# Moving the full-precision rows of odd blocks to ScalarE and the filter-half sums to VectorE in a diffusion transformer block

## Chip, cores and metric

The kernel runs on one core of one Trainium2 chip. The metric is the device time of one execution in microseconds, taken as the median of several runs.

## What is computed

One block of a hybrid diffusion model on 512 latent tokens and 256 context tokens of width 1024: an adaptive norm, one input projection whose columns feed four token mixers (differential attention, neighbourhood attention, pooling and a long convolution with generated filters), an output projection with a gate, and then a mixture of 16 experts with two of them per token. The change touches the norm with its modulation, and the generation of the convolution's filters:

```python
mod_l = jnp.split(jax.nn.silu(c) @ lp['ada_w'] + lp['ada_b'], 6, axis=-1)
mod_c = jnp.split(jax.nn.silu(c_ctx) @ lp['ada_w'] + lp['ada_b'], 6, axis=-1)
hl = rmsnorm(xl, lp['norm1_g']) * (1.0 + sc1_l) + sh1_l
hc = rmsnorm(xc, lp['norm1_g']) * (1.0 + sc1_c) + sh1_c
aq_l, ak_l, av_l, bq_l, bk_l, bv_l, pool_l, hy_l = split_cols(hl @ lp['w_in'])
...
h = jnp.sin(HY_SIN_FREQ * (h @ w2 + b2))
h = (h @ w3 + b3).reshape(L, HY_ORDER, 2, HY_CH)
h = h * jnp.exp(-t_norm[:, None, None, None] * deltas)
return h * lax.rsqrt(jnp.sum(h * h, axis=(0, 2), keepdims=True) + EPS)
```

The two halves of a filter (forward and backward) are needed as their sum and their difference, since the spectrum of the two-sided filter is built from those.

## The kernel before

Products are made to nearly full float32 precision from two reduced-precision parts: a number x is kept as hi (x rounded to fp32r) and lo (x minus hi, in fp32r), and a product takes three matmuls, hi by hi, hi by lo and lo by hi (`mm3`, lines 77 to 79). `split` (lines 72 to 74) makes the parts: ScalarE copies to hi, VectorE subtracts for lo.

The first 90 us hold these stages. `ada1` streams eight 1 MB pieces of the modulation weights through TensorE (line 355), moves each result out (line 358, ScalarE and VectorE in turn), and turns it into columns in the PSUM tile `pm` (line 360). From `pm`, VectorE makes the shift `md` and the scale `m1` (lines 362 to 364). `filters` generates the long convolution's filters for two orders n: a small network, the decay (line 287), the sums of squares `sqs` (line 292), then the sum `s` and the difference `d` of the two halves (line 301: GpSimd adds, VectorE subtracts), their splits `hs` and `hd`, the norm `ss` over partitions (line 306) with its root and reciprocal, and the transform to the spectrum (line 318, tiles `fk`), whose results VectorE scales (line 323) and GpSimd combines (lines 328 to 331).

`modulate` takes the normed tokens in eight blocks of 128 columns, first for the latents (`ht`, 512 wide), then for the context (`hc`, 256 wide). For each block TensorE transposes into a PSUM bank `xt` (line 373; four banks go round), ScalarE writes hi = scale * x + shift from PSUM (line 379), VectorE writes the same in full precision to the tile `hf` from the same bank (line 380; two `hf` buffers), and lo = hf - hi is made by VectorE in even blocks and by GpSimd in odd blocks (line 381). The first projection group (tiles `pl`, latents, and `pc`, context, lines 488 to 504) takes these parts block by block. The splits of its weights (`wh` on ScalarE, `wl` on VectorE, 2048 wide) lie on the same engines.

The order of the instructions on each engine isn't that of the text. The program is built with a scheduler that simulates a timeline and puts what it finds ready in front, so matmuls of the projection (written after `modulate`) run between the filter's and the transposes, and a changed duration or engine can change the order of other instructions, later ones too. What it puts on an engine then runs in that fixed order.

After the first 90 us come the rest of the projection with the convolution, the attentions, the output projection, the routing, and from about 460 us the experts, whose weights (line 1605, 1 MB pieces) stream in while TensorE works.

Of the kernel before, what the change touches and what calls it, by code (L numbers as in the profile page):

```python
# [11 lines left out]
AF = mybir.ActivationFunctionType  # L12
ALU = mybir.AluOpType
# [33 lines left out]
def tile_hybrid_block(ctx, tc, ins, out):  # L47
    nc = tc.nc
    V, A, G, T, SY = nc.vector, nc.scalar, nc.gpsimd, nc.tensor, nc.sync
# [19 lines left out]
    def f(ap):  # L69
        return ap.bitcast(F32)  # L70

    def split(hi, lo, src, eng=None):
        A.copy(hi, src)  # L73
        (eng or V).tensor_sub(lo, src, f(hi))  # L74
# [119 lines left out]
    def xbank(name, shape=(128, 512)):  # L194
        return psx.tile(list(shape), F32, tag="x", name=name, bufs=2)

    def jbank(name, shape=(128, 512)):
        return psx.tile(list(shape), F32, tag="j", name=name, bufs=2)

    def tbank(name, shape=(128, 512)):  # L200
        return pst.tile(list(shape), F32, tag="t", name=name, bufs=4)
# [66 lines left out]
    def filters():  # L268
        p = xbank("f1", (64, 512))
# [5 lines left out]
        p = xbank("f2", (64, 512))  # L275
# [5 lines left out]
        for n in range(2):  # L281
            hh = fw([128, 4, 2, 256], F32, "hh")
            sqs = fw([128, 2, 256], F32, "sqs")
            for j in range(4):
                p = xbank("f3")
# [12 lines left out]
            hsp = {nm: [fw([128, 4, 256], F32R, f"h{nm}{q}") for q in range(2)] for nm in "sd"}  # L298
            for nm, op in (("s", ALU.add), ("d", ALU.subtract)):
                t = fw([128, 4, 256], F32, "hsd")  # L300
                (G if nm == "s" else V).tensor_tensor(t, hh[:, :, 0, :], hh[:, :, 1, :], op=op)
                split(hsp[nm][0], hsp[nm][1], t)
            yield 1
            ss = xbank("ss", (128, 256))
# [6 lines left out]
            for ft in range(2):  # L311
                fwd = dftf[ft]
                pk = []
                for m in range(4):
                    p = xbank("fk", (128, 256))
# [11 lines left out]
                k = fw([128, 4, 256], F32, "kt")  # L327
# [14 lines left out]
    md = cst.tile([128, 16, 2], F32, name="md")  # L342
    m1 = cst.tile([128, 8, 2], F32, name="m1")
# [23 lines left out]
    def modulate(xs, vi):  # L367
        nt = len(xs)
        n = nt * 128
        for k in range(8):  # L370
            p = tbank("xt")
            for j in range(nt):
                T.transpose(p[:, j * 128:(j + 1) * 128], xs[j][:, k * 128:(k + 1) * 128], ident)
            hf = t1.tile([128, 512], F32, tag="hf", name="hf", bufs=2)
            if vi == 0:
                hi, lo = hT[0][k // 4][:, k % 4, :], hT[1][k // 4][:, k % 4, :]
            else:
                hi, lo = hC[0][:, k, :], hC[1][:, k, :]
            A.activation(hi, p[:, :n], AF.Identity, scale=m1[:, k, vi:vi + 1], bias=md[:, k, vi:vi + 1])
            V.tensor_scalar(hf[:, :n], p[:, :n], m1[:, k, vi:vi + 1], md[:, k, vi:vi + 1], op0=ALU.mult, op1=ALU.add)  # L380
            (G if k % 2 else V).tensor_sub(lo, hf[:, :n], f(hi))
            yield

    flt = filters()

    def some(g, n):
# [10 lines left out]
    hC = [hslot(4 + q, [128, 8, 256], f"hc{q}") for q in range(2)]  # L397
    xs_c = load_x(cd, 2, W1.ld[7])
    run(modulate(xs_l, 0))
    norm_x(xs_c)  # L400
    run(modulate(xs_c, 1))
    t1_s.close()
    sbank = tbank
# [691 lines left out]
    p = jbank("b16", (128, 16))  # L1095
# [123 lines left out]
    for k in range(2):  # L1219
        V.scalar_tensor_tensor(jg(oh[:, k]), jg(erk), float(k), gm.to_broadcast([128, 16, 4]), op0=ALU.is_equal,  # L1220
                               op1=ALU.mult)
# [208 lines left out]
    for r, t in g2p.items():  # L1430
        n = 128 // r
# [135 lines left out]
    for i, (t, c) in enumerate(steps):  # L1567
        k = (tiles[t][0], c)
# [137 lines left out]
    for i, (t, c) in enumerate(steps):  # L1706
        k = (tiles[t][0], c)
# [32 lines left out]
    big, n = [], len(chunks)  # L1740
# [48 lines left out]
    with tc.If(nxv > 0):  # L1789
# [25 lines left out]
        for nm, val in (("i", vid), ("g", vg)):  # L1815
            o_ = ow([128, 8, val.shape[2], NX], F32R, "ox" + nm)
            p = psm.tile([128, val.shape[2], NX], F32, tag="tp", name="px" + nm, bufs=2)
# [12 lines left out]
        for i in range(NX):  # L1830
# [3 lines left out]
            for c in range(6):  # L1834
                t = big[2]
# [174 lines left out]
```

## Time and profile before

| | |
|---|---|
| median of 3 runs | 743.69 us (741.64 to 745.98) |
| profiled execution | 739.1 us, of which the span of instructions 737.1 us |
| TensorE matmul busy | 652.6 us (89%) |
| VectorE busy | 369.5 us (50%) |
| ScalarE busy | 260.1 us (35%) |
| GpSimd busy | 135.5 us (18%) |
| HBM read and written | 176.08 MB and 21.11 MB |

The engines are named PE (TensorE, matmul), PEld (its weight loads), DVE (VectorE), ACT (ScalarE), POOL (GpSimd) and SP (the queue that issues most DMAs). A row of a timeline or of a group names the line of the kernel, the engine, the operation, the tile written and the tiles read, and the shapes. In brackets or behind the bar stands how long the engine had stood idle before, and what ended that. PE's busy time is stretched where one matmul waits for the next one's operands, so counts and the duration of one say more there than the sum.

### The profile page before, as it was taken

Reading aid. Unit: us, or ns where it says so; the run is one execution under the profiler, and the core shown is the slowest. Engines: PE = TensorE matmul, PEld = TensorE weight load, DVE = VectorE, ACT = ScalarE, POOL = GpSimd, SP = SyncE. Lnnn points to the kernel's source line nnn. Section 1 sums busy time; section 2 is a strip of 40 time slices with the busy share of each in tenths; the row PEclk is TensorE's granted clock in tenths of the full one; section 3 lists DMA queues with packets and bytes.
Section 4 is the critical chain, followed back from the end, with each engine's and each line's share of the span. In section 5 each row is a group of like instructions: output and inputs, shape, how many; then the busy total and the mean of one; then the engine's idle time right before and its main releaser. Section 6 shows DMA issues by size and latency. Waiting matters only on the chain.

```text
span 737.1 us, 10538 instructions
## 1 busy us (share of the span) xinstructions
PE 652.6 (89%) x3992; PEld 416.2 (56%) x3992; DVE 369.5 (50%) x699; ACT 260.1 (35%) x462; POOL 135.5 (18%) x129
## 2 busy tenths in 40 slices
PE   4879999999959899979899963999999999999791
PEld 1457777879947787667688842433344344432230
DVE  3699845787815876894745366131122222211136
ACT  3573414241215776668752170210110120110024
POOL 1027433231204500000000012011012222111112
PEclk9969999999979999878999985999999999999995
DMA  8972357764482663397601496999999999999983
GB/s 316 418 279 113 115 185 257 267 258 160 175 222 92 226 226 92 134 377 282 261 1 57 152 357 251 426 377 370 374 367 369 404 359 380 377 397 384 381 295 118
DMA packets 45915, 196.23 MB, mean 266 GB/s; under 512 B 6246, under 2 KB 12985, under 8 KB 28963
## 3 DMA queue, kind: packets, MB, share of 16 engines
q1 hardware_dynamic: 37322, 173.06, 62.3%
q0 software_dynamic: 7312, 18.63, 8.6%
q10 hardware_dynamic: 1224, 3.81, 1.3%
q8 instruction: 33, 0.54, 0.3%
q14 instruction: 24, 0.19, 0.1%
HBM read 176.08 MB, written 21.11 MB: 268 GB/s over the span
## 4 chain that ended last, share of the span: by engine, by line
PE 53%; DMA 8%; DVE 7%; ACT 4%; issue 2%; SPq 0%; ACTq 0%; DVEq 0%
PE h L1468 19%; PE y L1535 7%; DMA mw<-in_moe_w_dram 3%; PE poA L764 3%; PE pw L77 2%; PE pw L78 2%; PE pw L79 2%; PE y L1521 2%; PE tpx L1363 2%; DMA kst<-kd 2%; DMA xg<-hld,r_ids 1%; DVE wl L74 1%; PE tB L995 1%; PE tph L1493 1%; PE poB L1008 1%
## 5 line engine op out<-in xcount | busy, mean ns | idle before, releaser
L1468 PE MATMUL h<-mw,xT 128*32 128x256 f32 (+2 forms) x992 | 151.2, 480 | 4.8 <-DMA mw<-in_moe_w_dram 4.2
L1468 PEld LDWEIGHTS h<-mw,xT 128*32 128x32 f32 (+2 forms) x992 | 52.5, 125 | 91.0 <-issue 67.3
L1483 ACT ACTIVATE hs<-h 64x512 f32<-64x512 f32 (+2 forms) x22 | 11.2, 507 | 162.1 <-PE h L1468 120.0
L1535 PE MATMUL y<-mw,hx 128*32 128x256 f32 (+2 forms) x464 | 66.5, 465 | 0.0
L77 PE MATMUL pl<-ht,wh 128*128 128x512 f32 x128 | 52.8, 412 | 3.8 <-DVE bk L74 2.5
L78 PE MATMUL pl<-ht,wh 128*128 128x512 f32 x128 | 52.0, 407 | 0.0
L79 PE MATMUL pl<-ht,wl 128*128 128x512 f32 x128 | 51.8, 405 | 0.0
L1550 POOL DMA_INDIRECT xld<-ysb,r_ids x18 | 28.2, 1566 | 109.5 <-DMA xld<-ysb,r_ids 46.9
L1535 PEld LDWEIGHTS y<-mw,hx 128*32 128x32 f32 (+2 forms) x464 | 23.6, 123 | 34.0 <-issue 26.4
L74 DVE TENSOR_TENSOR wl<-raw,wh 128x2048 fp32r<-128x2048 f32 x14 | 33.4, 2389 | 14.8 <-ACT wh L73 14.8
L1370 ACT ACTIVATE xT<-tpx,mcol 128x128 f32<-128x128 f32 (+3 forms) x52 | 18.5, 440 | 53.6 <-PE tpx L1363 53.5
L775 DVE TENSOR_REDUCE ml<-s 128x1 f32<-128x768 f32 x32 | 30.3, 951 | 11.2 <-PE s L758 11.0
L776 ACT ACTIVATE eA<-s,ml 128x768 f32<-128x768 f32 x32 | 28.8, 903 | 19.2 <-DVE ml L775 14.4
L1484 DVE SCALAR_TENSOR_TENSOR hs<-hs,r_gsl,h 64x512 f32<-64x512 f32 (+1 forms) x13 | 9.7, 742 | 50.7 <-ACT hs L1483 35.2
L73 ACT CAST wh<-raw 128x2048 fp32r<-128x2048 f32 x14 | 26.7, 1908 | 20.5 <-DMA raw<-in_w_in_dram 18.2
L77 PEld LDWEIGHTS pl<-ht,wh 128*128 128x128 f32 x128 | 24.4, 191 | 10.3 <-DVE bk L74 2.7
L764 PE MATMUL poA<-aT,av 128*128 128x256 f32 x96 | 28.6, 456 | 1.1 <-ACT aT L804 0.8
L78 PEld LDWEIGHTS pl<-ht,wh 128*128 128x128 f32 x128 | 24.5, 191 | 6.8 <-issue 1.6
L79 PEld LDWEIGHTS pl<-ht,wl 128*128 128x128 f32 x128 | 24.5, 191 | 6.5 <-issue 1.3
L1048 DVE TENSOR_TENSOR xl<-pw,xl 128x512 f32<-128x512 f32 x24 | 16.5, 691 | 23.2 <-PE pw L79 23.0
L1178 POOL DMA_INDIRECT xg<-hld,r_ids x12 | 12.3, 1026 | 84.8 <-PE tpx L1363 75.2
L1368 DVE TENSOR_SCALAR xT<-tpx,mcol 128x128 f32<-128x128 f32 (+3 forms) x44 | 13.8, 376 | 27.0 <-PE tpx L1363 27.0
(462 smaller groups left out, 1423.8 us busy)
## 6 DMA issues: line engine op xcount, KB each, us to landing
mw<-in_moe_w_dram SPq DMA_DIRECT2D x92, 1024.0 KB, 8.7
raw<-in_ada_dram SPq DMA_DIRECT2D x24, 1024.0 KB, 5.0
raw<-in_w_in_dram SPq DMA_DIRECT2D x10, 1024.0 KB
raw<-in_w_out_dram SPq DMA_DIRECT2D x4, 1024.0 KB, 6.0
mw<-in_moe_w_dram SPq DMA_DIRECT2D x6, 512.0 KB, 10.4
mixd<-mx SPq DMA_DIRECT2D x5, 512.0 KB
kst<-kd SPq DMA_DIRECT2D x24, 96.0 KB, 2.2
xin<-in_x_dram SPq DMA_DIRECT2D x4, 512.0 KB, 11.7
```

What stands on the lines that cost most here:

```text
L73: A.copy(hi, src)
L74: (eng or V).tensor_sub(lo, src, f(hi))
L77: T.matmul(ps, a[0], b[0], start=start, stop=False)
L78: T.matmul(ps, a[0], b[1], start=False, stop=False)
L79: T.matmul(ps, a[1], b[0], start=False, stop=stop)
L764: T.matmul(po, avs[:, c, (h // 2) * 128:(h // 2 + 1) * 128], aT[:, c, :], start=(c == 0), stop=(c == 5))
L775: V.tensor_reduce(ml[:, cmp:cmp + 1], s[:, 0:768], axis=AX.X, op=ALU.min)
L776: A.activation(e[:, cmp, :], s[:, 0:768], AF.Exp, scale=-1.0, bias=ml[:, cmp:cmp + 1], accum_out=ml[:, 2 + cmp:3 + cmp])
L1370: A.activation(xT[:, k, :], p[:, i, :], AF.Identity, scale=sc, bias=sh)
L1468: T.matmul(p, xk, b, start=(k == 0), stop=(k == 7))
L1535: T.matmul(p, x[k], b, start=(k == 0), stop=(k == 3))
L1550: G.indirect_dma_start(out=dst_, out_offset=bass.IndirectOffsetOnAxis(ap=at_, axis=0), in_=y, in_offset=None, bounds_check=last_, oob_is_e ...
```

## The change

In `filters`, the sum of the two filter halves is made by VectorE, as the difference already was; before it was GpSimd. This is one instruction for each of the two orders n. In `modulate`, the full-precision row `hf` of the odd blocks (k = 1, 3, 5, 7) is made by ScalarE, with the operation that makes hi; before it was VectorE in all blocks. These are four instructions of 512 columns and four of 256. Who makes hi and lo stays as it was.

```diff
             for nm, op in (("s", ALU.add), ("d", ALU.subtract)):
                 t = fw([128, 4, 256], F32, "hsd")
-                (G if nm == "s" else V).tensor_tensor(t, hh[:, :, 0, :], hh[:, :, 1, :], op=op)
+                V.tensor_tensor(t, hh[:, :, 0, :], hh[:, :, 1, :], op=op)
                 split(hsp[nm][0], hsp[nm][1], t)
...
             A.activation(hi, p[:, :n], AF.Identity, scale=m1[:, k, vi:vi + 1], bias=md[:, k, vi:vi + 1])
-            V.tensor_scalar(hf[:, :n], p[:, :n], m1[:, k, vi:vi + 1], md[:, k, vi:vi + 1], op0=ALU.mult, op1=ALU.add)
+            if k % 2:
+                A.activation(hf[:, :n], p[:, :n], AF.Identity, scale=m1[:, k, vi:vi + 1], bias=md[:, k, vi:vi + 1])
+            else:
+                V.tensor_scalar(hf[:, :n], p[:, :n], m1[:, k, vi:vi + 1], md[:, k, vi:vi + 1], op0=ALU.mult,
+                                op1=ALU.add)
             (G if k % 2 else V).tensor_sub(lo, hf[:, :n], f(hi))
```

## Rows read from the trace of the kernel before

**Rows 1.** Busy time of each engine over the whole span, from the page.
```profile
PE 652.6 (89%) x3992; PEld 416.2 (56%) x3992; DVE 369.5 (50%) x699; ACT 260.1 (35%) x462; POOL 135.5 (18%) x129
```

**Rows 2.** Busy time by stretch: the columns are named in the first row.
```profile
core 0: us, PE busy (x) PEld busy (x) DVE busy (x) ACT busy (x) POOL busy (x), PEclk, DMA share, GB/s
35.00:46.70 11.70, 9.26 (x65) 5.96 (x56) 10.96 (x17) 8.81 (x12) 4.83 (x5) 0.65 1.04 387
46.70:73.10 26.40, 23.79 (x129) 18.92 (x129) 25.66 (x41) 12.81 (x19) 15.59 (x17) 0.90 0.37 132
75.50:145.00 69.50, 69.50 (x381) 53.94 (x380) 43.00 (x57) 21.65 (x27) 21.52 (x22) 1.00 0.57 205
460.00:700.00 240.00, 232.30 (x1631) 92.20 (x1631) 48.37 (x123) 30.93 (x76) 39.89 (x29) 0.99 1.01 382
46.70:52.80 6.10, 4.71 (x22) 4.32 (x23) 5.99 (x7) 5.93 (x7) 1.65 (x1) 0.55 0.61 203
```

**Rows 3.** Groups by shape, 44 to 78 us: xcount, busy us, mean ns, idle before.
```profile
L380 DVE TENSOR_SCALAR hf<-xt,m,md 128x512 f32<-128x512 f32 x8 | 6.3, 803 | 0.6 <-POOL ht L381 0.5
...
L379 ACT ACTIVATE ht<-xt,md,m 128x512 fp32r<-128x512 f32 x8 | 5.8, 783 | 2.7 <-PE xt L373 2.3 <-DVE m L364 0.4
...
L379 ACT ACTIVATE hc<-xt,md,m 128x256 fp32r<-128x256 f32 x8 | 4.2, 560 | 8.1 <-PE xt L373 8.1
...
L380 DVE TENSOR_SCALAR hf<-xt,m,md 128x256 f32<-128x256 f32 x8 | 4.2, 533 | 0.1
...
L381 POOL TENSOR_TENSOR ht<-hf,ht 128x512 fp32r<-128x512 f32 x4 | 6.3, 1567 | 13.4 <-DVE hf L380 13.4
```

**Rows 4.** The same view on PE alone, 45.2 to 75.5 us.
```profile
L373 PE MATMUL xt<-ca,xin 128*128 128x128 f32 x36 | 7.0, 328 | 1.2 <-DVE hf L380 0.8 <-DVE md L362 0.4
...
L78 PE MATMUL pc<-hc,wh 128*128 128x256 f32 x8 | 3.7, 457 | 0.8 <-DVE hc L381 0.8
...
L77 PE MATMUL pc<-hc,wh 128*128 128x256 f32 x8 | 2.2, 280 | 0.0
```

**Rows 5.** Timeline of the filter sums, 35 to 47 us: start us, us, instruction.
```profile
35.08 0.68 DVE L292 TENSOR_TENSOR sqs<-sqs,sq 128x512 f32<-128x512 f32 x1
...
35.25 2.72 POOL L301 TENSOR_TENSOR hsd<-hh 128x1024 f32<-128x1024 f32 x1 [31.93 <-DVE hh L287]
...
36.01 2.51 DVE L292 TENSOR_TENSOR sqs<-sqs,sq 128x512 f32<-128x512 f32 x1
...
36.69 1.07 PE L355 MATMUL ad<-raw,sl 128*32 128x256 f32 x16
...
37.93 2.15 POOL L295 DMA_DIRECT2D fwd<-in_dftf_dram  x4
...
38.67 2.04 PE L306 MATMUL ss<-sqs,ca 128*128 128x256 f32 x4 [0.91 <-DVE sqs L292]
...
39.08 1.23 DVE L74 TENSOR_TENSOR hs<-hsd,hs 128x1024 fp32r<-128x1024 f32 x1 [0.56 <-ACT hs L73]
...
40.22 1.22 DVE L301 TENSOR_TENSOR hsd<-hh 128x1024 f32<-128x1024 f32 x1
...
41.29 1.93 PE L355 MATMUL ad<-raw,sl 128*32 128x256 f32 x16
...
44.48 1.88 ACT L73 CAST wh<-raw 128x2048 fp32r<-128x2048 f32 x1
...
46.60 0.17 DVE L364 TENSOR_TENSOR m<-m,vec 128x16 f32<-128x16 f32 x1
```

**Rows 6.** The same instructions for the second order, from the timeline, 66 to 86 us.
```profile
75.89 2.54 DVE L292 TENSOR_TENSOR sqs<-sqs,sq 128x512 f32<-128x512 f32 x1
...
84.29 1.03 PE L306 MATMUL ss<-sqs,ca 128*128 128x256 f32 x4
```

**Rows 7.** The chain that ended last, 185 to 210 us: start us, us, what.
```profile
193.21 2.76 DVE wl L74
...
195.99 4.77 DMA raw<-in_ada_dram
```

## Prediction

> **What bounds the kernel now.** I read the busy shares of the page first [rows 1]. The reader is to see that PE leads with 652.6 us of the 737.1 us span and that DVE, with half of the span, isn't the bound on average. So the change, which takes work from DVE and POOL, can only be worth something in a stretch where DVE ends last. Both edits lie in the first 85 us, so the second view is the busy time by stretch [rows 2]. From 46.7 to 73.1 us, the modulation, DVE is busy for 25.66 of 26.40 us, ACT for 12.81, POOL for 15.59. That is a stretch that DVE sets, though PE is not far behind (23.79, stretched by waits). From 35 to 46.7 us, the filter sums and the last pieces of the modulation weights, DVE is busy for 10.96 of 11.70 us, and PE's granted clock averages 0.65. From 75.5 to 145 us PE is busy without a gap (69.50 of 69.50): there DVE sets nothing, and what is gained or lost before 75.5 us is handed on as a shift. From 460 to 700 us the weight stream has a DMA share of 1.01 and PE is busy for 232.30 of 240 us. That stretch can't become shorter, but it starts when the stages before it end, so a shift passes through it too.
>
> **Edit 1, the sum of the filter halves.** Removed is a POOL instruction of 2.72 us from 35.25 to 37.97 us; added is a DVE instruction, whose twin, the difference, takes 1.22 us at the same shape [rows 5]. The row to look at is the DVE addition into `sqs` at 36.01: 2.51 us, where the same instruction took 0.68 us at 35.08 [rows 5]. It ends at 38.52, 0.55 us behind the POOL instruction, and the second order shows it again (2.54 us at 75.89) [rows 6]. So a DVE operation of two SBUF inputs stood still while POOL worked, and without the POOL sum it should take 0.68 us. In DVE's queue that is 1.22 more for the sum, 2.51 - 0.68 = 1.83 less for `sqs`, and the 0.56 us that DVE stood idle before the split of `hs`, waiting on ACT behind POOL's sum, can go too. The sum is 1.22 - 1.83 - 0.56 = -1.17 us, so I take a gain of 1.2 us. It lies on the path that starts the modulation: the scale `m1` is ready only when DVE reaches line 364 at 46.60, after all this in its queue. What is late next is DVE again, with the reciprocal and the two splits. The lower bound is 0: the planner may put the freed time behind line 364. The upper bound takes in PE's clock, which was at its upper level when 16 matmuls of line 355 took 1.07 us at 36.69, and at the lower (1.2 of 2.4 GHz) when they took 1.93 at 41.29, after PE had stood 0.91 us for `sqs` [rows 5]. The `ss` matmuls took 2.04 us there and 1.03 us at the second order [rows 5, 6]. Were the clock to stay up, 0.86 + 1.01 = 1.9 us come on top, 3.1 us in all.
>
> At the second order the same trade is worth 0.64 us on DVE (1.22 us more against 2.54 - 0.68 = 1.86 less [rows 5, 6]) and I cost it at nothing on the path, since PE is busy without a gap from 75.5 us and reaches `ss` only at 84.29 [rows 2, 6]. Were that cover gone, it would be a gain of 0.64, not a cost.
>
> POOL's queue also holds the four issues of the transform matrices behind the sum (37.93) [rows 5]. They can move up by at most 2.72 us, and would then share a DMA that is full (share 1.04 [rows 2]) with the first projection weight, whose ACT cast at 44.48 waited for no transfer [rows 5]. I cost that at nothing. Without that cover the cast, and the first `pl` matmul behind it, are late by up to 2.7 us.
>
> **Edit 2, the full-precision rows of odd blocks.** DVE loses four instructions of 0.803 us and four of 0.533 us, ACT gains four of about 0.783 and four of about 0.560, by its own rows with the same input, scale and shift (only the output is float32) [rows 3]. That is 5.3 us off DVE and 5.4 us onto ACT. Over the stretch DVE falls to 25.66 - 5.3 = 20.4 us and ACT rises to 12.81 + 5.4 = 18.2 of 26.4 us [rows 2], so neither is full any more and PE would set the pace.
>
> What PE can take of the 5.3 us is bounded by what it lost to DVE. PE waited 0.8 us for `hf` to free banks before transposes, and 0.8 us for the lo parts of `hc` [rows 4]. A wait also hides in stretched matmuls: the eight `pc` matmuls of line 78 that first take a lo part average 457 ns, those of line 77 beside them 280, so 8 x 0.177 = 1.4 us. That makes 0.8 + 0.8 + 1.4 = 3.0 us. I take the `hc` part, 0.8 + 1.4 = 2.2 us, as gained, since there ACT is idle before line 379 for 8.1 us in all, and can take the four small rows [rows 3]. I do not take the 0.8 us before the transposes: they fall from 46.7 to 52.8 us, where ACT is busy for 5.93 of 6.10 us [rows 2], and up to three of the large rows come into its queue there. The bounds: at best all 5.3 us of DVE's relief; at worst ACT delays the hi parts by three large rows, 3 x 0.783 = 2.3 us, a loss.
>
> The wait that is added: ACT's odd row needs the `hf` buffer that POOL's subtraction two blocks earlier read, 1.567 us long [rows 3]. Behind a waiting ACT stand the hi parts of the next blocks, and PE's matmuls wait for those. Before, DVE waited for this, 0.5 us in all [rows 3]. I keep 0.5 us inside the worst case above, since ACT's blocks stand further apart than DVE's.
>
> A rule of the Trainium skill speaks against this edit: ScalarE: Activation LUTs, Rules for kernel authors, has multiplications and additions on VectorE rather than ScalarE, as up to about three times faster there in bf16. Here the two engines' rows for float32 from PSUM differ by 0.02 us [rows 3], so the trace does not bear it out for this shape. By the rule at its full factor the eight instructions would be, as an estimate, some 16 us on ACT, more than its free 13.6 us in the stretch, and edit 2 would cost about 2 us instead of giving 2.2.
>
> **The sum.** 1.2 + 2.2 = 3.4 us. The profiled execution was 739.1 us (span 737.1 and 2.0 us around it), so it would become 735.7. The median of the runs, 743.69, lies 0.6% above it; 3.4 us less is 740.3 us, which I predict. I count differences of over 0.5%, 3.7 us, as faster or slower; that is about what a measurement of this kernel can tell from no change, and the forecast lies just inside.
>
> **The rivals.** (A) All goes well: the clock stays up in the filter sums (3.1 us) and PE gains all of DVE's relief (5.3 us). That is 8.4 us, 735.3 us. For it speaks that DVE is the one full engine from 46.7 to 73.1 us; against it that PE named only 3.0 us of waits for DVE there.
> (B) ACT takes DVE's place in 46.7 to 52.8 us. The 1.2 us of edit 1 are gained, and edit 2 gives between +0.5 and -2.3 us: 742.0 to 744.8, say 743.4 us. For it speaks the 5.93 of 6.10 us [rows 2]; against it that the planner knows of ACT's load and can put the weight cast of 1.9 us later.
> (C) Slower: the planner's new order puts a 2048-wide weight split in front of a short DVE operation on the chain, late in the projection. One such place is on the chain before: the split at 193.21 takes 2.76 us and the transfer whose buffer it frees 4.77 us more [rows 7], 7.5 us for a place of that kind. With the 3.4 us gained it ends at 743.69 + 4.1 = 747.8 us. Decisive is whether a further place costs over 3.4 us; past 7.1 us it is slower by more than 0.5%. For it speaks that every instruction behind the edits may be ordered anew; against it that the first half of the program only shifts as a whole.
> That the change does not do what it says cannot be: both edits fix the engine.
>
> **How the numbers follow.** Forecast 0.40 (of which 0.24 gain over 3.7 us and 0.16 less), A 0.17, B 0.19, C 0.24 (0.20 slower by over 0.5%, 0.04 within). So faster 0.24 + 0.17 = 0.41, same 0.16 + 0.19 + 0.04 = 0.39, slower 0.20. The range reaches from a little beyond A, 734.5, to C, 748: both ends hold about a tenth outside.
>
> **What would show it right or wrong.** Edit 1 is right if the `sqs` addition of the first order takes about 0.7 us and line 364 comes at about 45.4 instead of 46.6. Edit 2 is right if the `pc` matmuls of line 78 fall from 457 towards 280 ns and the first `pl` of the gapless stretch comes at about 72 instead of 75.5 us. If DVE is still full from 46 to 72 us, or ACT is, B holds. If the start of the gapless stretch is 3 us earlier and the end is not, the gain went to another order later (C), and the place is where the two timelines' shift changes. Wrong in size would be the clock: if PE stays at its upper level from 40 to 52 us, A.

## The result, and the profile after

The changed kernel took 745.96 us (median of 20 runs, 741.49 to 750.01) against 741.01 us for the kernel before (20 runs, 735.58 to 746.34). The ratio is 1.0073, interval 1.0052 to 1.0094, so the change makes the kernel some 5 us slower. The predicted 740.3 us is missed on the other side; the time lies within the range, near rival C. Part of the distance is the base: the three runs shown had a median of 743.69, the twenty 741.01. The profiled execution of after took 749.75 us (span 747.7), that of before 739.1. They lie 3.8 us above and 1.9 us below their medians, so their difference of 10.6 us isn't what the change costs.

The busy shares of the page of after, to be read against [rows 1]:

```profile
PE 654.0 (87%) x3992; PEld 417.8 (56%) x3992; DVE 364.8 (49%) x693; ACT 264.8 (35%) x470; POOL 134.4 (18%) x127
```

The work went where it was sent: DVE 4.7 us less, ACT 4.7 us more, POOL two instructions less. PE issues the same 3992 matmuls. The loss isn't work but waiting, so the next view is the busy time by stretch of after, columns as in [rows 2]:

```profile
35.00:46.70 11.70, 6.55 (x63) 4.71 (x60) 11.36 (x18) 9.89 (x16) 0.98 (x2) 0.91 1.05 408
46.70:73.10 26.40, 23.78 (x136) 19.62 (x134) 21.98 (x33) 17.40 (x27) 19.26 (x19) 0.91 0.30 105
75.50:145.00 69.50, 69.48 (x372) 53.73 (x371) 42.82 (x59) 22.00 (x26) 20.83 (x23) 1.00 0.59 213
145.00:160.00 15.00, 7.97 (x44) 5.31 (x46) 13.27 (x20) 7.01 (x7) 7.33 (x6) 0.91 0.53 193
160.00:165.00 5.00, 5.00 (x27) 3.34 (x28) 2.08 (x3) 1.09 (x2) 0.00 (x0) 0.60 0.79 279
```

and of before the last two of these stretches:

```profile
145.00:160.00 15.00, 13.27 (x78) 10.57 (x77) 14.91 (x23) 7.15 (x9) 7.04 (x7) 1.00 0.66 247
160.00:165.00 5.00, 5.00 (x42) 4.03 (x41) 2.72 (x4) 1.31 (x2) 0.00 (x0) 1.00 0.92 351
```

In the modulation DVE fell from 25.66 to 21.98 us, and up to 145 us nothing is lost. Then PE runs 44 matmuls in 15 us where it ran 78, and the clock averages 0.60 behind it, where it was 1.00.

The reading that finds such a place is a map of shifts: each matmul of after is paired with the same matmul of before (the same line and tiles, counted in order), and the median difference of their starts is taken by stretch. Where the order differs, single matmuls lie several us to either side of that median. For after it is -2.77 us at 80 to 140 us, +4.34 at 162 to 175, and +5.74 at 340 to 360. So there was an early gain not far from the predicted 3.4 us (of what it is made is told below), it was carried for 65 us, and 7.1 us were lost in one place, between 145 and 162 us. By the rows above, PE stood idle for 7.03 of the 15 us instead of 1.73; that is 5.3 us, and the other 1.8 us, as an estimate, go with the lower clock behind the idle time. Here is that place before, from the timeline (start us, us, instruction, idle time before it and what ended that):

```profile
152.76 1.08 ACT L597 COPY hb<-pl 128x512 f32<-128x512 f32 x1
153.63 2.82 DVE L74 TENSOR_TENSOR wl<-raw,wh 128x2048 fp32r<-128x2048 f32 x1
...
156.51 0.39 PE L78 MATMUL pn<-wl,ht 128*128 128x256 f32 x1 [1.71 <-DVE wl L74]
...
159.89 1.05 ACT L73 CAST ysp<-yt 128x1024 fp32r<-128x1024 f32 x1 [5.21 <-DVE yt L668]
```

and after (line numbers behind 380 are 4 higher):

```profile
154.74 3.50 POOL L673 TENSOR_TENSOR yt<-yr 128x256 f32<-128x256 f32 x1
155.04 0.41 DVE L672 TENSOR_TENSOR yt<-yr 128x256 f32<-128x256 f32 x1
155.38 2.28 DVE L74 TENSOR_TENSOR wl<-raw,wh 128x2048 fp32r<-128x2048 f32 x1
158.27 1.04 ACT L73 CAST ysp<-yt 128x1024 fp32r<-128x1024 f32 x1 [6.96 <-POOL yt L673]
159.22 1.05 ACT L601 COPY hb<-pl 128x512 f32<-128x512 f32 x1
...
159.37 0.58 PE L77 MATMUL pz<-ysp,inv 128*128 128x256 f32 x1 [7.03 <-ACT ysp L73]
159.88 1.94 PE L422 MATMUL ad<-raw,sl 128*32 128x512 f32 x8
...
161.75 0.58 PE L77 MATMUL pn<-wh,ht 128*128 128x256 f32 x1
```

Two strands meet there: the projection (matmuls `pn`, which need the weight split `wl` and a PSUM bank that ACT frees by copying `pl` to `hb`), and the convolution (sums of the second spectrum into `yt`, their split `ysp`, the inverse transform `pz`). Before, the projection goes first on all three engines, and its matmuls cover the convolution's sums. After, each of three queues has the convolution first: on DVE the split `wl` stands behind the sums, on ACT the copy `hb` stands behind the cast of `ysp`, on PE `pz` stands ahead of the next `pn`. PE stood for 7.03 us at `pz` with projection matmuls queued behind it. POOL's last sum, which the cast waits for, took 3.50 us beside the split.

### The profile page after: what moved, and what is told of

It is laid out like the page before. It is cut to its first block, busy times and chain, and to the rows that moved or that the text cites. A ratio compares the mean times of both kernels' runs of the same rounds, so it can differ in the third digit from the quotient of the medians.

```text
span 747.7 us, 10530 instructions
## 1 busy us (share of the span) xinstructions
PE 654.0 (87%) x3992; PEld 417.8 (56%) x3992; DVE 364.8 (49%) x693; ACT 264.8 (35%) x470; POOL 134.4 (18%) x127
## 5 line engine op out<-in xcount | busy, mean ns | idle before, releaser
L1472 PE MATMUL h<-mw,xT 128*32 128x256 f32 (+2 forms) x992 | 148.4, 476 | 0.0
L1539 PE MATMUL y<-mw,hx 128*32 128x256 f32 (+2 forms) x464 | 70.1, 482 | 1.7 <-DVE hx L1499 1.7
```

What stands on the lines that cost most here:

```text
L1472: T.matmul(p, xk, b, start=(k == 0), stop=(k == 7))
L1539: T.matmul(p, x[k], b, start=(k == 0), stop=(k == 3))
```

## The experiments

No experiment changes what is computed. Each was timed beside runs of the kernel before on the same chip, with medians from 739.88 to 741.33 us, and the ratio is to those runs. Shifts (us) are those of the map above, from one profiled execution each, whose starts vary by some 1 us (that of p1_early took 745.36 us, 7.0 above its median):

| kernel | median us | ratio (95%) | shift 80-140 | 162-175 | 340-360 | `wl` starts | `hb` and cast of `ysp` |
|---|---|---|---|---|---|---|---|
| before | 741.01 | 1 | 0 | 0 | 0 | 153.63 | `hb` first |
| after | 745.96 | 1.0073 (1.0052-1.0094) | -2.8 | +4.3 | +5.7 | 155.38 | `hb` behind |
| e1_sum | 746.28 | 1.0080 (1.0050-1.0110) | +4.3 | +1.7 | +5.5 | 154.86 | behind |
| e2_hf | 745.81 | 1.0052 (1.0025-1.0079) | -4.2 | +4.0 | +6.5 | 154.16 | behind |
| g1_pe | 747.98 | 1.0103 (1.0076-1.0130) | -2.4 | +4.3 | +7.0 | 155.79 | behind |
| g2_wl | 743.41 | 1.0027 (1.0000-1.0054) | -3.2 | +2.2 | +2.9 | 154.21 | first |
| g4_lock | 745.66 | 1.0067 (1.0042-1.0093) | -2.9 | +3.8 | +5.5 | 156.19 | behind |
| b1 | 750.01 | 1.0117 (1.0085-1.0149) | -1.2 | +4.4 | +11.4 | 155.20 | first |
| g5_early | 746.08 | 1.0085 (1.0060-1.0111) | -3.7 | -2.2 | +5.1 | 151.72 | first |
| g6_es | 743.93 | 1.0050 (1.0027-1.0072) | -4.0 | -2.6 | +3.5 | 150.58 | first |
| p1_early | 738.35 | 0.9965 (0.9945-0.9985) | -2.8 | -3.8 | -1.0 | 150.23 | first |
| p2_es | 735.84 | 0.9936 (0.9908-0.9963) | -2.7 | -4.7 | -1.3 | 149.16 | first |
| p3_b1 | 743.92 | 1.0045 (1.0019-1.0070) | -0.8 | +4.1 | +6.5 | 155.59 | first |
| p4_e2 | 737.89 | 0.9953 (0.9934-0.9973) | -3.3 | -4.1 | -1.6 | 149.55 | first |
| p7_before | 738.80 | 0.9957 (0.9929-0.9985) | +0.9 | -0.9 | +0.5 | 152.73 | first |
| p8_e1 | 742.01 | 1.0027 (0.9995-1.0059) | +1.9 | -1.4 | +1.0 | 152.45 | first |
| p0_after | 738.17 | 0.9961 (0.9934-0.9989) | -2.3 | -4.3 | -0.6 | 150.16 | first |
| f1_old | 742.43 | 1.0039 (1.0008-1.0069) | -0.9 | +2.1 | +3.1 | 154.20 | first |
| f1_hf | 741.14 | 1.0032 (1.0004-1.0060) | -2.4 | +0.1 | +1.2 | 152.71 | first |
| f2_wl | 746.38 | 1.0098 (1.0064-1.0132) | -2.8 | +6.0 | +6.4 | 152.94 | behind |

### Each edit alone

**e1_sum**: edit 1 without edit 2.

```diff
-                (G if nm == "s" else V).tensor_tensor(t, hh[:, :, 0, :], hh[:, :, 1, :], op=op)
+                V.tensor_tensor(t, hh[:, :, 0, :], hh[:, :, 1, :], op=op)
```

> Only the first edit: both sums of the filter halves on VectorE, all full-precision rows stay on VectorE. Order theory (the early stages gain, and the loss comes where a 2048-wide weight split now stands behind the second spectrum's last sums, near 155 us): here the planner keeps that split ahead of those sums, as in the kernel before, so only the early gain is left: about 1 us faster than the kernel before, ratio 0.998, PE's longest wait between 140 and 165 us below 3 us. Rival (the work that was moved is itself dearer): the sums on VectorE cost what the changed kernel lost, ratio 1.003 or more.

Measured 1.0080: a miss. Between 145 and 165 us PE's longest wait is 0.8 us (below 3 was expected), but the shift is -2.9 us at 40 to 46 us and then +4.3 at 80 to 140: the loss lies within the modulation. Its timeline shows the weight splits there:

```profile
49.21 3.38 DVE L74 TENSOR_TENSOR wl<-raw,wh 128x2048 fp32r<-128x2048 f32 x1
...
54.29 3.26 DVE L74 TENSOR_TENSOR wl<-raw,wh 128x2048 fp32r<-128x2048 f32 x1
```

Before, the same two started at 46.68 and 51.84 and took 2.28 and 2.45 us. Now they stand among the `hf` rows and beside POOL's work, and PE waits 3.4 us in all for `hf` where it waited 0.8 [rows 4]. So edit 1 alone meets rival C too, at another place.

**e2_hf**: edit 2 without edit 1.

```diff
+            if k % 2:
+                A.activation(hf[:, :n], p[:, :n], AF.Identity, scale=m1[:, k, vi:vi + 1], bias=md[:, k, vi:vi + 1])
+            else:
...
```

> Only the second edit: full-precision rows of odd blocks on ScalarE, the first sum of the halves stays on GpSimd. Order theory: the planner puts the split behind the second spectrum's last sums here too, as in the changed kernel, so PE stands some 7 us for ysp near 155 us; 5 to 7 us slower than the kernel before, ratio 1.007 to 1.010. Rival (the moved work is dearer): the loss shows as VectorE's or ScalarE's time before 75 us, and the first 75 us are no shorter than before.

Measured 1.0052, which is below the range of 1.007 to 1.010, with the largest early gain of all (-4.2) and a loss like that of after at 145 to 162 us (to +4.0). Here too `hb` stands behind the cast and PE waits 7.0 us at `pz`, as expected. The shift is still -0.3 us at 46 to 60 us, so nearly all of the early gain comes between there and 80 us: with the order that it got, edit 2 shortened the modulation by more than the 2.2 us forecast. Each edit alone costs about as much as both together, so the loss isn't a sum of what the edits do.

### One queue put back at a time

**g2_wl**: after, with two of the second spectrum's sums put behind the split on DVE.

```diff
+    behind(mark["s3", 0, 1], W2.wl[at[2]], False)
+    behind(mark["s12", 0, 1], W2.wl[at[2]], False)
```

> The changed kernel, with two sums of the second spectrum of the first order (yr, lines 668 and 669) ordered behind the weight split on VectorE, without a wait between engines. Order theory: PE can start the pn matmuls at about 154.5 instead of 162 us and doesn't stand for ysp; 6 to 9 us faster than the changed kernel, so 1 to 4 us faster than the kernel before, ratio 0.995 to 0.999. Rival (the loss belongs to the moved work): nothing comes back, ratio 1.006 to 1.008.

**g4_lock**: after, with POOL's last sum made by DVE.

```diff
-            G.tensor_add(t[:, 3], yr[:, 1], yr[:, 3])
+            (V if n == 0 and ft == 1 else G).tensor_add(t[:, 3], yr[:, 1], yr[:, 3])
```

> The changed kernel, with the last sum of the second spectrum of the first order (line 673) made by VectorE instead of GpSimd, so that it can't stand still beside the split; the split stays behind the spectrum. If GpSimd's 3.5 us at that sum are the whole loss: ysp is ready some 2.5 us earlier, PE's wait falls from 7.0 to about 4.5 us, ratio about 1.003. If the order of the split is the larger part, as I think, 4 us of wait are left and the time is still 2 to 4 us above the kernel before.

**g1_pe**: after, with `pz` put behind the projection matmuls on PE.

```diff
+    behind(mark["pz", 0, 0, 1, 0], mark["pn", 2, 0, 7], False)
```

> The changed kernel with one thing altered, on PE alone: the first pz product that needs the second spectrum stands behind the pn products instead of ahead of them, so that pn can start when the weight split is done (157.7 us) and not when the spectrum is (159.4 us). Theory (the stall is made of two orders, VectorE's and PE's): PE's wait shrinks from 7.0 to about 5.5 us and is put down to the weight split, and 1 to 3 us come back: ratio to before 1.003 to 1.006. Rival (the late spectrum itself is what the following work needs): ratio stays at 1.006 to 1.009.

g2_wl gives back 2.2 us at 162 us and 0.46% in time, some 3.4 us where 6 to 9 were expected; here the planner also put `hb` first. From its timeline:

```profile
152.68 1.04 ACT L601 COPY hb<-pl 128x512 f32<-128x512 f32 x1
...
156.54 0.39 PE L78 MATMUL pn<-wl,ht 128*128 128x256 f32 x1 [3.81 <-DVE wl L74]
```

PE now waits for the split alone, since the split itself still comes at 154.21. g4_lock takes POOL's 3.50 us away and `pz` starts 1.9 us earlier,

```profile
157.44 0.58 PE L77 MATMUL pz<-ysp,inv 128*128 128x256 f32 x1 [4.41 <-ACT ysp L73]
```

and PE's wait falls to the 4.4 us expected, but the shift behind it is still +3.8 and the time 1.0067: the stretched sum is at most a small part of the loss. g1_pe, a miss, isn't faster than after (1.0103 against 1.0073). PE's waits from 145 to 165 us (engine, line, waited for: us in total, times, longest) show what stood in its way:

```profile
PE ad L422 <- DMA raw<-in_ada_dram: 5.6, 1, 5.6
```

The `ad` matmuls behind the last `pl` wait for a transfer whose buffer the late split frees, and `pn` then waits for `hb` behind the cast. PE's queue alone back in place is of no use while the other two stay as they are.

### The late order put into the kernel before, and the early one into after

**b1**: before, with the split behind the sums on DVE and the first `pn` behind the first `pz` of ft = 1 on PE.

```diff
+    behind(W2.wl[at[2]], mark["vb", 0, 1], False)
+    behind(mark["pn", 2, 0, 0], mark["pz", 0, 0, 1, 0], False)
```

> The kernel before, with nothing of the change in it, but with the changed kernel's order at 150 to 160 us laid on it: the third weight split (wl) behind all of VectorE's sums of the second spectrum, and the first pn product behind the first pz product that needs the second spectrum. Theory (the order at that place costs the time): PE waits some 6 to 8 us for the cast of that spectrum instead of 1.7 us for the weight split, and the kernel comes out 4 to 9 us slower than before, ratio 1.005 to 1.012. Rival (the loss belongs to the work moved onto ScalarE and VectorE, and the order is only how it shows): ratio within 0.998 to 1.003.

**g5_early**: after, with the split ahead of all the sums of the second spectrum.

```diff
+    [behind(mark[x], W2.wl[at[2]], False) for x in (("p4", 0, 1), ("s0", 0, 1), ("s12", 0, 1),
+                                                    ("ca", 1, 0), ("cb", 1, 0))]
```

> The changed kernel with the third weight split put still further forward, behind the fourth product of the second spectrum and ahead of all its sums and of the first pair of x2c sums. Its cast was done at 150.8 us in the changed kernel, so the split should end near 154 us instead of 157.7, PE's wait for it should be 1.5 to 2.5 us instead of 7.0 (3.8 where only two sums were put behind it), and the shift at 165 us should be within 1.5 us of the kernel before. Theory: ratio to before 0.998 to 1.003, below the 1.0027 of the variant with two sums behind the split. Rival (VectorE is full from 136 to 162 us, so what the split gains the spectrum loses, and PE waits for that instead): ratio 1.002 to 1.006.

**g6_es**: g5_early, with the copies `es` of the first order on ACT instead of DVE.

```diff
-            V.tensor_copy(es, pe)
+            (A.copy if n == 0 else V.tensor_copy)(es, pe)
```

> As the variant with the weight split put furthest forward, and besides the two copies es<-pe of the first hyena spectrum pair (VectorE, 0.68 us each) made by ScalarE, which is idle there. If VectorE's full stretch of 136 to 162 us sets the time, 0.7 to 1.4 us come back on top of that variant: ratio to before 0.996 to 1.001. If PE's products set it, nothing is added: the two variants agree within 0.7 us.

b1 came out as expected in time, though PE waits 3.9 us at `pz` and not 6 to 8. g5_early missed; g6_es took 0.35% less than g5_early, but missed its range too. The map says why the times mislead. In g5_early and g6_es the place is mended (shift -2.2 and -2.6 at 162 us), and then 6.4 and 4.6 us are lost between 225 and 360 us, in the attention, which no edit touches; b1 loses 7.4 us there too. PE's waits from 240 to 345 us, of before, b1 and g5_early:

```profile
PE s L757 <- ACT eA L776: 1.8, 4, 0.6
```

```profile
PE s L757 <- ACT eA L776: 7.6, 6, 3.9
```

```profile
PE s L761 <- ACT eA L780: 7.2, 5, 3.9
```

These variants gave the planner new times, and it reordered the attention as well. after itself doesn't lose there (+5.8 before, +5.7 behind). So the variants had to be compared with that stage held.

### With the attention's order held

In the p-kernels each engine takes the attention's instructions (lines 745 to 1010 of before) in the order that they have in before. GpSimd's first instruction of those lines stands early, so its queue is held from near the program's start.

```diff
+    for s in PIN.values():
+        names = ["I-" + n for n in s.split() if "I-" + n in ix]
+        for a, b in zip(names, names[1:]):
+            tc.add_manual_dep(ix[b], a, mybir.DependencyInfo(mybir.DependencyClass.NoSync, mybir.DependencyReason.DATA), ...)
```

**p1_early**: g5_early so held. 

> The changed kernel with the third weight split put forward as in g5_early, and from the first attention product on (line 757 of before, about 215 us) every engine held to the order of the kernel before. g5_early was ahead of the kernel before by 1 to 2 us up to 250 us and then lost 6 to 7 us between 250 and 340 us, where the planner had given it another order of the attention products. Theory (the change pays 2 us by itself, and all that it lost, it lost to two reorderings): ratio to before 0.995 to 1.000, ahead by 1 to 2 us at 300 us. Rival (the loss of 250 to 340 us comes from something else than order, such as transfers that start at other times): ratio 1.004 to 1.009 again.

**p2_es**: g6_es so held. 

> As p1_early, with the two copies es<-pe of the first pair on ScalarE as in g6_es. Theory: 0.3 to 1 us faster than p1_early, ratio to before 0.993 to 0.999. Rival (order isn't it): ratio 1.003 to 1.007, as g6_es.

**p3_b1**: b1 so held. 

> The kernel before with the changed kernel's order at 150 to 160 us, as b1, and the attention held to the order of before. b1 was 10 us slower, of which 5 stood at 165 to 240 us and the rest came between 240 and 340 us. Theory: only the first 5 us stay, ratio to before 1.005 to 1.009. Rival (the second loss follows from being late, not from the order): ratio 1.011 to 1.015 again.

**p4_e2**: edit 2 alone, with the early split, so held. 

> Edit 2 alone (the full-precision rows of odd blocks on ScalarE; the filter sums as before), with the weight split put forward and the attention held to the order of before. It tells whether edit 2 pays by itself once both orders are taken out: theory 1.5 to 4 us faster than before, ratio 0.994 to 0.999, at most 1 us from p1_early. If edit 1 is worth its own 1.2 us, it comes out slower than p1_early by about that.

p1_early falls from 1.0085 to 0.9965 and its wait for `eA` from 7.2 to 3.1 us; p2_es is the fastest kernel of the study. p3_b1 is the clean counterpart: the kernel before with two queues turned. Its order is that of before up to 150 us. It goes from -0.8 to +4.1 us at the place, PE waits there for the cast as it does in after,

```profile
157.38 0.39 PE L77 MATMUL pz<-ysp,inv 128*128 128x256 f32 x1 [3.94 <-ACT ysp L73]
```

and it takes 0.45% (0.19 to 0.70) more time, a little less than expected. Another 2.4 us come up to 340 to 360 us (+6.5); p7_before below, which is held in the same way, takes on 1.4 us there too (-0.9 to +0.5). So the late order alone, without either edit, makes the kernel slower. p4_e2 agrees with p1_early (0.9953 and 0.9965): with the early split, edit 1 adds nothing to edit 2 that can be seen (an estimate from the two intervals: -0.9 us, give or take 2).

**p7_before**: the kernel before with the early split, held. 

> The kernel before, with nothing of the change, but with the weight split put forward in the same way as in p1_early (behind the fourth product of the second spectrum and ahead of all its sums and of the first pair of x2c sums), attention held to its own order. It tells what in p1_early's 2.7 us belongs to the change and what to the better place of the split. Theory (in the kernel before the split stood only two short sums and one x2c pair later, and PE waited 1.7 us for it): at most 1 to 2 us faster, ratio to before 0.9975 to 1.000, so that the change itself keeps 1 to 2 us. Rival (all of p1_early's gain is the split's place, and the change pays nothing): ratio 0.995 to 0.998.

**p8_e1**: edit 1 alone with the early split, held. 

> Edit 1 alone (filter sums on VectorE), with the split put forward and the attention held as in p1_early. Edit 1 alone lost 4 us at 60 to 80 us, where VectorE is full and the planner put a second 2048-wide split in front of the modulated rows. Theory (that place loses 4 us and nothing later takes it back): about 3 to 4 us slower than p7_before, ratio to before 1.001 to 1.005. Rival (edit 1 is worth its 1.2 us once the later orders are as before): 0.995 to 0.998.

**p0_after**: after, held, with no other constraint. 

> The changed kernel with only the holding of the attention order added; its order was the same as before there already, so its instructions stand as in the changed kernel on every engine. It is the control of the holding itself. Theory: as the changed kernel, ratio to before 1.004 to 1.009. Rival (the holding by itself makes the kernel faster): below 1.002.

p7_before, without either edit, is as fast as p1_early with both: 0.9957 and 0.9965. So with the early split the two edits are worth nothing that can be measured: 0.6 us slower with an uncertainty of some 2.5 us, which leaves room for a gain of 2 us but not for the 3.4 forecast. p7_before differs from before in order alone, on DVE from 150 us and on PE from 161 us on, and is 0.43% (0.15 to 0.71) faster. p8_e1 gains nothing over before; the modulation, whose order isn't held, takes back its early gain as expected (-3.0 us at 40 to 46 us, +1.9 at 80 to 140). p3_b1 and p7_before are one kernel but for the order of DVE and PE from 150 us on and what follows from it on ACT, and they lie 0.9% apart.

p0_after was meant as a control that keeps the loss, and missed: 0.9961. With POOL's queue held from near the start, the planner's order differs from that of after from about 60 us on, and in that order the place is free:

```profile
150.16 2.82 DVE L74 TENSOR_TENSOR wl<-raw,wh 128x2048 fp32r<-128x2048 f32 x1
151.33 1.11 ACT L601 COPY hb<-pl 128x512 f32<-128x512 f32 x1 [0.69 <-PE pl L79]
...
156.74 1.05 ACT L73 CAST ysp<-yt 128x1024 fp32r<-128x1024 f32 x1 [3.46 <-DVE yt L672]
```

PE is busy there for 14.96 of the 15 us from 145 to 160. As a control it failed; as a comparison it says most: the same two edits, the same instructions, another order, and 738.17 instead of 745.96 us. By the ratios, the order is worth 1.1%, about 8 us.

### With the whole order held

What would the edits be worth had the planner not reordered anything? In the f-kernels each engine's whole queue is held by the same code.

**f1_old**: both edits, each queue in the order of before. 

> The changed kernel with every engine and queue held to the order of the kernel before over the whole program up to the experts: both edits, no reordering. The moved rows stand on ScalarE right behind the cast-making activation of the same block, the moved sums on VectorE right behind the last product they need. This is the world in which the prediction's sum was made. Theory (the sum of the edits was about right and the planner's reordering is the whole miss): 2 to 5 us faster than before, ratio 0.993 to 0.998. Rival (the edits are worth nothing by themselves; p0_after, p1_early and p7_before agree within 0.6 us): 0.998 to 1.002. Second rival (the edits cost time): above 1.003.

**f1_hf**: edit 2 alone, the same. 

> Edit 2 alone (rows of odd blocks on ScalarE), every engine held to the order of the kernel before. The prediction gave it 2.2 us of 3.4. Theory: 1 to 3 us faster than before, ratio 0.996 to 0.9985, and slower than f1_old by 0.5 to 2 us. Rival (VectorE's time is not what bounds 45 to 75 us once the order is fixed): 0.999 to 1.002.

**f2_wl**: after in its own order, with the split early and `pz` and `ad` behind `pn`. 

> The changed kernel with its own order held everywhere, but for three things at 150 to 165 us: the third weight split stands behind the last product of the second spectrum instead of behind all its sums, and on PE the one pz product that needs that spectrum and the ada product that waits for a transfer stand behind the pn products instead of ahead of them. Nothing else in the program moves. Theory (this place is the whole loss): 5 to 8 us come back, ratio to before 0.995 to 1.001, against 1.007 of the changed kernel. Rival (other new orders lose as much): ratio above 1.003.

All three missed. f1_old has before's order on PE to the last matmul, and it isn't faster but 0.39% slower. So my sum, which priced the edits in that order, was wrong by itself. First the early stages. The timeline of f1_old at the first weight cast of the modulation:

```profile
50.50 0.78 ACT L381 ACTIVATE hf<-xt,md,m 128x512 f32<-128x512 f32 x1 [0.61 <-DVE ht L385]
51.18 1.90 ACT L73 CAST wh<-raw 128x2048 fp32r<-128x2048 f32 x1
...
53.11 2.29 DVE L74 TENSOR_TENSOR wl<-raw,wh 128x2048 fp32r<-128x2048 f32 x1 [1.92 <-ACT wh L73]
...
56.06 0.50 PE L78 MATMUL pl<-ht,wh 128*128 128x512 f32 x1 [1.59 <-DVE ht L385]
```

The row that went to ACT waits for a buffer and stands ahead of the cast, which started at 49.47 in before. The split and the lo rows behind it are late, and PE waits 1.59 us. Edit 1 is no better in that order. The VectorE sum stands ahead of the copy `adr` that PE needs for `pm`, and DVE waits later for the root that ACT takes of `ss`:

```profile
36.74 0.61 PE L360 MATMUL pm<-sel,adr 128*128 128x2 f32 x4 [1.31 <-DVE adr L358]
40.90 1.75 DVE L309 RECIPROCAL rn<-rn 128x256 f32<-128x256 f32 x1 [1.07 <-ACT rn L308]
```

By the same rows of before PE waited 0.18 us for `adr`, then 0.91 us for `sqs` [rows 5], and DVE's reciprocal waited for nothing; now PE waits 1.31 us and nothing, and DVE 1.07. By 80 to 140 us f1_old has -0.9 us, as much as its start differs already at 10 to 30 us (-0.7). f1_hf shows -2.4, but -2.8 of it was there at 40 to 46 us, ahead of edit 2, which itself gave +0.4. So in the old order both edits are worth nothing in the early stages.

The 0.39% comes later, at the known place, though no queue of the old order was turned there: between 145 and 162 us f1_old goes from -0.9 to +2.1 us and f1_hf from -2.4 to +0.1. In f1_old,

```profile
148.70 0.43 DVE L659 TENSOR_TENSOR yr<-uu,kt 128x256 f32<-128x256 f32 x1 [1.53 <-DMA kt<-kspec]
...
157.06 0.39 PE L78 MATMUL pn<-wl,ht 128*128 128x256 f32 x1 [2.48 <-DVE wl L74]
```

DVE waits 1.53 us for the spectrum `kt`, which in before had landed when DVE came to it, the split is late by about that, and PE waits 2.48 us for it where it waited 1.71. Behind that the granted clock falls. Before and f1_old (columns as in [rows 2]):

```profile
157.00:160.00 3.00, 3.00 (x28) 3.00 (x27) 3.00 (x5) 0.11 (x1) 2.06 (x2) 1.00 0.59 203
```

```profile
157.00:160.00 3.00, 2.94 (x16) 2.94 (x17) 3.00 (x6) 0.00 (x0) 1.98 (x2) 0.62 0.75 251
```

f1_hf shows the same with 0.82 us, 1.99 us and 0.64. So a gain made before 145 us didn't pass this place even in the old order; why `kt` landed late there is open.

f1_hf gained those first microseconds where it differs from before in nothing, which led back to all the traces. Take the shift from 10 to 30 us to 40 to 46 us, and the granted clock from 34 to 40 us. In before, e2_hf, p3_b1, p7_before and f1_old the clock is 0.85 to 0.91 and the shift between -0.2 and +0.4 us. In the other fifteen it is 1.00 and the shift -1.7 to -2.8 us. Three of the fifteen don't have edit 1: b1 with -2.1, p4_e2 with -1.7, f1_hf with -1.8. So some 2 us of the early gain is TensorE's clock, which stayed up in one execution and fell in another. With the clock up, the kernels with edit 1 show -1.8 to -2.8 us and the three without it -1.7 to -2.1, so by these executions edit 1's own part is a few tenths of a us. Whether edit 1 makes the higher clock likelier is open: with it in the planner's own order all twelve have it, of the other eight three.

f2_wl comes back to the place. Its split is early (152.94), and `pz` stands behind `pn`; only ACT still has the cast first:

```profile
159.71 1.04 ACT L73 CAST ysp<-yt 128x1024 fp32r<-128x1024 f32 x1 [6.32 <-POOL yt L673]
160.66 1.04 ACT L601 COPY hb<-pl 128x512 f32<-128x512 f32 x1
...
161.75 0.28 PEld L77 LDWEIGHTS pn<-wh,ht 128*128 128x128 f32 x1 [8.61 <-ACT hb L601]
```

PE stands for 8.4 us behind a copy of 1 us that frees a PSUM bank and is queued behind a cast that waits. That costs more than the two other queues gave: the shift at 162 us is +6.0 where after has +4.3. In all kernels of the table with `hb` behind the cast the shift at 162 us is +1.7 to +6.0; where `hb` is first and the split starts by 152.8 it is -4.7 to +0.1. Moving `hb` alone was not tried.

## Why the prediction was wrong

**Right: where the work goes and what it costs.** The second `sqs` addition and line 364 in after's timeline:

```profile
36.80 0.68 DVE L292 TENSOR_TENSOR sqs<-sqs,sq 128x512 f32<-128x512 f32 x1
...
43.77 0.15 DVE L364 TENSOR_TENSOR m<-m,vec 128x16 f32<-128x16 f32 x1
```

It fell from 2.51 to 0.68 us as worked out. Line 364 came at 43.77, not 45.4. The clock averaged 0.91 from 35 to 46.7 us instead of 0.65, the extra of 1.9 us that I had put into rival A only; the size is right, but b1, p4_e2 and f1_hf have it without edit 1. The rows of edit 2, and the matmuls that take the lo parts, from the groups by shape of after, 44 to 78 us:

```profile
L383 DVE TENSOR_SCALAR hf<-xt,m,md 128x512 f32<-128x512 f32 x4 | 3.2, 806 | 1.3 <-POOL ht L385 1.2
L381 ACT ACTIVATE hf<-xt,md,m 128x512 f32<-128x512 f32 x4 | 3.2, 796 | 4.2 <-POOL ht L385 4.2
L78 PE MATMUL pc<-hc,wh 128*128 128x256 f32 x8 | 2.9, 358 | 0.6 <-DVE hc L385 0.5
L381 ACT ACTIVATE hf<-xt,md,m 128x256 f32<-128x256 f32 x4 | 2.3, 565 | 2.8 <-DVE hc L385 2.4 <-POOL ht L385 0.4
```

ACT's rows take 0.796 and 0.565 us against the 0.783 and 0.560 predicted, and DVE's wide ones 0.806. The Trainium skill's preference for VectorE, which it gives for bf16 (ScalarE: Activation LUTs, Rules for kernel authors), isn't borne out for this shape. The `pc` matmuls of line 78 went halfway, from 457 to 358 ns, which is 0.8 of the 1.4 us counted on. The added wait, ACT for the `hf` buffer behind POOL, is 4.2 us in the wide rows, where I had kept 0.5.

**Wrong, first: "what is gained or lost before 75.5 us is handed on as a shift".** The step held to 145 us and no further: 7.1 us were lost between 145 and 162. It took for granted that the order behind the edits would stay, though the planner can change it with any changed duration, as the description of the kernel says. The argument that I held against rival C, that the first half only shifts as a whole, is what failed. It failed in the old order too, where f1_hf lost the 2.4 us that it had.

**Rival C was the case.** I gave it 0.24 and a price of 7.5 us for one place; the place cost 7.1. That the two are so near is luck: my price was that of a split and a transfer, the place's is idle time of PE and a lower clock. Its mechanism was close in kind, not in form: not a long split ahead of a short operation, but three queues that all put the convolution before the projection, with the split and a short copy behind. p3_b1 shows two of them sufficient in the kernel before, f2_wl that ACT's queue holds the loss when the other two are back in place.

**Wrong, second: the sum of 3.4 us itself.** It priced each edit in before's order, where f1_old and f1_hf, one execution each, show it to be worth about 0 by 140 us. For edit 1 the failing step is that DVE's queue alone set line 364. DVE did get its 1.83 us back, but with its sum ahead of `adr` PE's wait moves from `ss` to `pm`, and DVE then waits 1.07 us behind PE and ACT. For edit 2 the failing term is the 1.4 us of stretched `pc` matmuls, which I took for a wait on DVE though no row names one. In f1_old, as in f1_hf, they are hardly shorter:

```profile
L78 PE MATMUL pc<-hc,wh 128*128 128x256 f32 x8 | 3.5, 442 | 0.0
```

That is 0.1 us instead of 1.4. The named waits for `hf` and `hc`, 0.8 us each, are gone, but PE now waits 0.5 us for ACT's `hc`, and 1.6 us for `ht` in the wide blocks (1.8 in f1_hf). The latter is rival B's mechanism, which I had bounded but left out of the sum. In after itself, 2.3 us of the shift come up to 46 us with the clock at 1.00, and from there to 80 to 140 us, where edit 2 should have given 2.2, it is 0.5. That their total came near the forecast is a coincidence. p1_early and p7_before show the same from the other side: they differ by both edits, the shift between them is 3.7 us at 80 to 140 us, but 1.7 of that is there at 10 to 30 us and 3.4 by 40 to 46, and the medians agree.

**The better kernel.** p2_es (both edits, the split early, `es` on ACT, the attention held) takes 735.84 us: 0.64% under before (0.37 to 0.92), some 1.4% under after by the ratios. p7_before has 0.43% of it without either edit, and the two intervals overlap.

## What to carry to other kernels

Where a planner orders the queues, price an edit in the order that it will get, not in the one that the trace shows: build both, compare the queues, and look for a long split, or a short copy that frees a PSUM bank, which now stands behind something that waits. Read two traces by a map of shifts, since the cause is to be looked for where a shift jumps, and that may lie 80 us behind the edit. Before comparing variants, hold the order of the stages that they don't touch; here order alone was worth 8 us, and the two edits nothing that could be measured.

## What the runs showed of the hardware

A DVE instruction with two SBUF inputs and a POOL instruction that reads SBUF held each other up here. `sqs` took 2.51 us beside POOL's sum and 0.68 without it. The other way round, POOL's 128x256 sum took 3.50 us in after, where it ended 0.58 us behind DVE's 2.28 us split, and 0.92 us in p0_after. The Trainium skill says so (SBUF — State Buffer, Who interferes with whom: the shared port pair is an exclusive lock, and such an operation contends with GpSimd's reads); the rows agree. What I had not expected is how little it mattered: g4_lock takes the 3.50 us away and gains nothing that can be measured (1.0067 against 1.0073).

TensorE's clock adds its own scatter. The same work in the same order, at 366 to 375 us, in before and in p1_early (columns as in [rows 2]):

```profile
369.00:372.00 3.00, 3.00 (x17) 2.64 (x17) 1.92 (x5) 2.44 (x5) 0.00 (x0) 0.89 0.00 0
372.00:375.00 3.00, 3.00 (x17) 2.49 (x16) 1.60 (x4) 2.42 (x6) 0.00 (x0) 1.00 0.00 0
```

```profile
369.00:372.00 3.00, 3.00 (x10) 2.45 (x10) 1.71 (x3) 2.02 (x5) 0.00 (x0) 0.50 0.00 0
372.00:375.00 3.00, 3.00 (x10) 2.40 (x9) 0.15 (x1) 0.44 (x3) 0.00 (x0) 0.50 0.00 0
```

One came back to its upper level and the other ran on at the lower (0.50, 1.2 of 2.4 GHz), with 10 matmuls in 3 us instead of 17. In p1_early, p4_e2 and after that is a jump of 3.1 us against before, p2_es and p3_b1, which no edit made. With the 2 us of the clock at 34 to 40 us, that is the size of the whole effect under study: an effect of this size is read from the medians and from where a map of shifts jumps, not from two spans.
